# Moving some matmul operands to other start addresses in SBUF, relative to the weights loaded beside them

## The chip, the core and the metric

The kernel runs on one core of a Trainium2 chip. The metric is the device time of one execution in microseconds (us). The engines are called PE (TensorE, matmuls), DVE (VectorE), ACT (ScalarE), POOL (GpSimd) and SP (SyncE, which here only issues DMAs). "PEld" is the part of TensorE that loads weights: each matmul first has its stationary operand (128 columns) loaded, and while one matmul streams its moving operand, the weights of the next are already being loaded. All of it is read from SBUF, 128 partitions wide; an address below is a byte address within a partition.

## The reference

One layer of a decoder trunk, sequence 512, width 1024, 16 heads of 64, all in float32:

```
hn = rms_norm(x); proj = hn @ w_in                     # 1024 -> 3462 columns: q, k, v, forget logits, gate
q, k = rms_norm per head
o_moba = block-sparse attention (4 heads)              # y_moba = rms_norm(o)
cum    = cumsum(log_sigmoid(f_logit))                  # forget sums, 6 heads
o_fox  = softmax(q k / 8 + cum_q - cum_k) v (6 heads)  # y_fox = rms_norm(o) * sigmoid(gate)
o_dil  = mixture of three dilated windows (6 heads)    # y_dil = rms_norm(o)
x = x + concat(y_moba, y_fox, y_dil) @ w_out
x = x + square(relu(rms_norm(x) @ w_up)) @ w_down      # 1024 -> 4096 -> 1024
```

## The kernel before

Every product keeps float32 accuracy by splitting each operand into a rounded part ("hi", type fp32r) and the rest ("lo"). A product is then three matmuls per tile pair: hi by hi, hi by lo, lo by hi. The class `Stream` brings the weights in by DMA (`wraw`, or `ublk` for the up blocks), and `split_group` makes `whi` on ACT (L118) and `wlo` on DVE (L119), two pieces ahead of use.

There are four stages on PE, in this order.

- **In projection and attention** (10 to 236 us of the span). `product` (L274) multiplies x, split into `xh` and `xl`, with nine column chunks of `w_in`. Here x is the stationary operand (128 tokens at a time) and `whi` or `wlo` is the moving one, 512, 256, 262 or 384 columns wide. Between its matmuls a planner puts the steps of the attention heads: transposes (L495, L541, L580), scores (L514, L519), values (L565). DVE and ACT do the softmax and the splits.
- **Out projection** (L274 too). The weights `whi`, `wlo` are stationary and the normed attention outputs move, 512 columns: `y0h`/`y0l`, `y1h`/`y1l`, `y2h`/`y2l` for the three groups.
- **First block of the up projection** (`up0`, L274): the weights are stationary, `zh`/`zl` (the normed-to-be x) move, 512 columns.
- **The MLP** (L872 and L913, 315.7 to 634 us). For seven further blocks of the up projection the kernel uses seven products instead of eight on quarters of 256 columns (a Strassen scheme): products 1, 2, 3 and 4 move a quarter of `zh`/`zl`, products 5, 6 and 7 move a sum of quarters, `t5h`/`t5l`, `t6h`/`t6l`, `t7h`/`t7l`. Each product is 24 matmuls in `up_product` (L872). Between them stand the items of the down projection, `down_item` (L913): 24 matmuls of 512 columns which move `h`, the squared activations, as `hh0`, `hl0`, `hh1`, `hl1`. One round is: product 1, product 5, item, 2, 6, item, 3, 7, item, 4, item. There are seven rounds and then the last items alone: 28 products on `zh`/`zl` (672 matmuls), 21 on the sums (504) and 32 items (768).

The order of instructions on PE is the order in which the code is written. Tiles come from pools (`tile_pool`). A pool on the left takes addresses upward after the pools still open there, a pool with `side="right"` downward from the top. So the start of each tile follows from the sizes of all tiles opened before it. Forget sums: `cumulate` transposes the log gates, scans them along the sequence into the tile `cum` (6 partitions of 512, 2048 bytes of every partition) and writes them to DRAM; `bias_tiles` reads one row back for each of the six heads, spread over 128 partitions, into a tile `ck` of a pool with two buffers.

Of the kernel before, what the change touches and what calls it, by code (L numbers as in the profile page):

```python
# [11 lines left out]
F32 = mybir.dt.float32  # L12
# [6 lines left out]
P = 128  # L19
D = 1024  # L20
S = 512
# [4 lines left out]
NFOX = 6  # L26
# [130 lines left out]
def hymba_block(ctx: ExitStack, tc: tile.TileContext, a, out):  # L157
# [4 lines left out]
    small = ctx.enter_context(tc.tile_pool(name="small", bufs=2))  # L162
# [5 lines left out]
    def bank(tag):  # L168
        return psum.tile([P, 512], F32, name=tag, tag=tag)
# [77 lines left out]
    def product(first, ks, operands, banks_n, done, G=2):  # L247


        n = len(ks)  # L250
        acc = [None] * banks_n
        head, tail = list(range(min(G, n))), list(range(max(G, n - G), n))
        mid = [k for k in range(n) if k not in head and k not in tail]
        order = [(k, b) for b in range(banks_n) for k in head]
        order += [(k, b) for k in mid for b in range(banks_n)]
        order += [(k, b) for b in range(banks_n) for k in tail]
        if first == 0:

            wh, wl = w.take(0)
            acc = [bank("acc") for _ in range(banks_n)]  # L260
            for m in (0, 2, 1):
                for b in range(banks_n):
                    pairs, view = operands(ks[0], b, wh, wl)
                    lhs, rhs = pairs[m]
                    nc.tensor.matmul(view(acc[b]), lhsT=lhs, rhs=rhs, start=(m == 0), stop=False)
            order = [(k, b) for k, b in order if k > 0]
        for k, b in order:
            wh, wl = w.take(first + k)
            if acc[b] is None:
                acc[b] = bank("acc")  # L270
            pairs, view = operands(ks[k], b, wh, wl)
            dst = view(acc[b])
            for m, (lhs, rhs) in enumerate(pairs):
                nc.tensor.matmul(  # L274
                    dst, lhsT=lhs, rhs=rhs, start=(k == 0 and m == 0), stop=(k == n - 1 and m == 2)
                )
            if k == n - 1:
                done(b, acc[b])
            yield
# [11 lines left out]


    p1 = ExitStack()
    xpool = p1.enter_context(tc.tile_pool(name="xpool", bufs=1))
    tokp = p1.enter_context(tc.tile_pool(name="tokp", bufs=5))
    att_stack = ExitStack()
    att = att_stack.enter_context(tc.tile_pool(name="att", bufs=2, side="right"))
# [156 lines left out]
    def cumulate():  # L454
        pt = bank("m")
        for u in range(NT):
            nc.tensor.transpose(out=pt[:NFOX, u * P : (u + 1) * P], in_=lf[:, u], identity=ident)
        cum = small.tile([NFOX, S], F32, name="cum", bufs=1)
        one = ones[:NFOX, :1].broadcast_to([NFOX, S])
        nc.vector.tensor_tensor_scan(cum, one, pt[:NFOX], 0.0, op0=ALU.mult, op1=ALU.add)  # L460
        nc.gpsimd.dma_start(cum_d, cum)
# [177 lines left out]
    for h in range(16):  # L639
        if h % 4 == 0:  # L640
            i = h // 4
            step(("root", i, 0), qk_parts[i][1], [(("qk", i), "root")])
            for t in range(NT):
                step(("norm", i, t), partial(qk_parts[i][2], t), [(("root", i, 0), "zero")] + ([(("norm", i, t - 1), "each")] if t else []))
        for m in range(2):
            needs = [(("norm", h // 4, t), "qk") for t in range(NT)] + [(("s", h - 3, i), "free") for i in range(NT)]
            if h >= FOX0:
                needs.append((("f", 0, 0), "zero"))
            step(("stack", h, m), stack_step(h, m), needs)
        for i in range(NT):  # L650
            needs = [(("stack", h, m), "stack") for m in range(2)] + [(("pt", h - 2, b), "free") for b in range(3)]
            if h >= FOX0:
                needs.append((("f", 0, 0), "cum"))
            step(("s", h, i), s_step(h, i), needs)
        for b in range(3):
            needs = [(("s", h, i), "s") for i in {i for _, i in BANKS[b]}] + [(("av", h - 1, 1), "free")]
            step(("pt", h, b), pt_step(h, b), needs)
        for half in range(2):
            needs = [(("pt", h, b), "pt") for b in range(3)] + [(("v", h // 4), "v")]
            step(("av", h, half), av_step(h, half), needs)  # L660
        step(("o", h, 0), o_step(h), [(("av", h, 1), "av"), (("o", h - 1, 0), "free")])
        if h + 1 == GROUPS[0][1]:
            for t in range(NT):
                step(("y", 0, t), partial(y_transpose, 0, t), [(("o", h, 0), "norm")])
        if h == 15:
            step(("sig", 0, 0), gate, [(("s", 15, NT - 1), "zero"), (("g", 0), "zero")])
        if h == FOX0 - 2:
            step(("f", 0, 0), cumulate, [(("v", 2), "f")])
# [53 lines left out]
    for k in range(0, NK, 2):  # L722
        nc.sync.dma_start(
            x2[:, k : k + 2], a["xT"][k * P : (k + 2) * P, :].rearrange("(k p) t -> p k t", p=P)
        )
    p2 = ExitStack()
    ypool = p2.enter_context(tc.tile_pool(name="ypool", bufs=1))
    for g in (1, 2):
        yT[g] = [ypool.tile([P, 3, S], F32R, name=f"y{g}{m}") for m in "hl"]
# [60 lines left out]


    tp = ctx.enter_context(tc.tile_pool(name="tsums", bufs=1))
    HALF = S // 2
    lo4, hi4, t0, t1 = slice(0, 4), slice(4, 8), slice(0, HALF), slice(HALF, S)
    zop = {1: (zh[:, lo4, t0], zl[:, lo4, t0]), 2: (zh[:, hi4, t0], zl[:, hi4, t0]), 3: (zh[:, hi4, t1], zl[:, hi4, t1])}
    tsum = {}

    def t_sum(n):
        t = mlp_pools["sum"].tile([P, 4, HALF], F32, name="wsum")
        first, second = {  # L800
            5: (zf[:, lo4, t1], zf[:, lo4, t0]),
            6: (zf[:, hi4, t1], tsum.get(5)),
            4: (zf[:, hi4, t0], tsum.get(6)),
            7: (zf[:, hi4, t1], zf[:, lo4, t1]),
        }[n]
        nc.vector.tensor_tensor(t, first, second, op=ALU.subtract)
        tsum[n] = t
        if n == 4:

            hi, lo = zh[:, lo4, t1], zl[:, lo4, t1]  # L810
        else:
            hi, lo = (tp.tile([P, 4, HALF], F32R, name=f"t{n}{m}") for m in "hl")
        zop[n] = (hi, lo)
        return n

    def t_split(n):
        hi, lo = zop[n]
        nc.scalar.copy(hi, tsum[n])
        nc.vector.tensor_tensor(lo, tsum[n], hi.bitcast(F32), op=ALU.subtract)
# [15 lines left out]
    def h_tiles(u):  # L835
        for p in range(2):
            h_at[u, p] = [hp.tile([P, 2, S], F32R, name=f"h{m}{p}", bufs=2) for m in "hl"]

    def square(c, hi, lo, rows=None):

        nc.vector.scalar_tensor_tensor(c, c, 0.0, c, op0=ALU.max, op1=ALU.mult)
        if rows is not None:
            nc.vector.tensor_tensor(c, c, rows, op=ALU.mult)
        nc.scalar.copy(hi, c)
        nc.vector.tensor_tensor(lo, c, hi.bitcast(F32), op=ALU.subtract)
# [13 lines left out]
    def up_product(u, n):  # L859
# [8 lines left out]
        for f in range(2):  # L868
            for j in range(4):
                lh, ll = (x[:, j, f * P : (f + 1) * P] for x in (wh, wl))  # L870
                for m, (lhs, rhs) in enumerate(((lh, bh[:, j]), (lh, bl[:, j]), (ll, bh[:, j]))):
                    nc.tensor.matmul(  # L872
                        acc[:, f * HALF : (f + 1) * HALF], lhsT=lhs, rhs=rhs,
                        start=first and (f, j, m) == (0, 0, 0), stop=(f, j, m) == (1, 3, 2), skip_group_check=True,
# [9 lines left out]
    def up_parts(u, n, acc):  # L884
# [10 lines left out]
        hi, lo = (x[:, :, cols] for x in h_at[u, p])  # L895
        rows = rv[:, cols].unsqueeze(1).broadcast_to([P, 2, HALF]) if u == 7 else None
        square(c.rearrange("p (f t) -> p f t", f=2), hi, lo, rows)
# [30 lines left out]
    for n, _ in enumerate(product(up0_first, list(range(NK)), up_operands, 4, up_done)):  # L928
        if n in (8, 13, 18):
            m = {8: 5, 13: 6, 18: 7}[n]  # L930
            t_sum(m), t_split(m)
        if n == 20:
            t_sum(4)
            zstack.close()
            hp = ctx.enter_context(tc.tile_pool(name="hp", bufs=1, side="right"))
            h_tiles(0)
    t_split(4)
    for u in range(1, 9):
        if u < 8:
# [80 lines left out]
```

## Time and profile before

| | us |
|---|---|
| median of 3 runs | 640.49 (640.24 to 640.78) |
| the profiled execution, its own time | 639.8 |
| its span, first to last instruction | 638.0 |
| PE busy in it | 627.6 |
| DVE busy | 460.2 |
| ACT busy | 322.4 |

[...]

### The profile page before, as it was taken

Reading aid. Unit: us, or ns where it says so; the run is one execution under the profiler, and the core shown is the slowest. Engines: PE = TensorE matmul, PEld = TensorE weight load, DVE = VectorE, ACT = ScalarE, POOL = GpSimd, SP = SyncE. Lnnn points to the kernel's source line nnn. Section 1 sums busy time; section 2 is a strip of 40 time slices with the busy share of each in tenths; the row PEclk is TensorE's granted clock in tenths of the full one; section 3 lists DMA queues with packets and bytes.
Section 4 is the critical chain, followed back from the end, with each engine's and each line's share of the span. In section 5 each row is a group of like instructions: output and inputs, shape, how many; then the busy total and the mean of one; then the engine's idle time right before and its main releaser. Section 6 shows DMA issues by size and latency. Waiting matters only on the chain.

```text
span 638.0 us, 9834 instructions
## 1 busy us (share of the span) xinstructions
PE 627.6 (98%) x3800; PEld 556.3 (87%) x3800; DVE 460.2 (72%) x786; ACT 322.4 (51%) x575; POOL 43.9 (7%) x63
## 2 busy tenths in 40 slices
PE   7999999999999999999999999999999999999997
PEld 5798898898889998888888989898988989988986
DVE  6794695696688565678899676686578765966872
ACT  7457666676777575549543433343434343433320
POOL 4010210130120100002100000000000000000000
PEclk9999999999999999999999999999999999999999
DMA  8524423323422345167425233422530333212213
GB/s 313 161 96 133 123 84 76 125 75 116 134 63 71 106 136 155 51 230 175 107 72 164 84 111 100 131 68 67 166 100 22 144 100 133 66 37 64 67 43 123
DMA packets 24911, 70.03 MB, mean 110 GB/s; under 512 B 3210, under 2 KB 4762, under 8 KB 24864
## 3 DMA queue, kind: packets, MB, share of 16 engines
q1 hardware_dynamic: 18224, 57.84, 28.5%
q10 hardware_dynamic: 4432, 5.77, 3.7%
q0 software_dynamic: 2208, 5.79, 3.7%
q8 instruction: 30, 0.49, 0.3%
q14 instruction: 17, 0.14, 0.1%
HBM read 61.51 MB, written 2.11 MB: 100 GB/s over the span
## 4 chain that ended last, share of the span: by engine, by line
PE 77%; DVE 7%; ACT 1%; issue 1%; ACTq 0%; POOL 0%; DVEq 0%
PE acc L913 28%; PE m L872 22%; PE acc L274 20%; PE m L514 2%; PE m L565 2%; PE m L541 1%; DVE ptl L548 1%; PE m L495 1%; DVE qkss L400 1%; DVE wlo L119 1%; DVE qks L418 1%; DVE m L526 1%; DVE qkraw L413 1%; DVE qkv L401 1%; DVE osum L582 0%
## 5 line engine op out<-in xcount | busy, mean ns | idle before, releaser
L118 ACT CAST whi<-wraw 128x1024 fp32r<-128x1024 f32 (+3 forms) x66 | 66.7, 1014 | 90.5 <-PE acc L913 39.9
L274 PE MATMUL acc<-whi,xh 128*128 128x512 f32 (+3 forms) x284 | 103.4, 364 | 0.7 <-DVE fl L436 0.4
L913 PE MATMUL acc<-hh,wlo 128*128 128x512 f32 x256 | 101.5, 396 | 0.0
L913 PE MATMUL acc<-hh,whi 128*128 128x512 f32 x256 | 101.3, 396 | 0.0
L913 PE MATMUL acc<-hl,whi 128*128 128x512 f32 x256 | 101.2, 395 | 0.0
L119 DVE TENSOR_TENSOR wlo<-wraw,whi 128x1024 fp32r<-128x1024 f32 (+3 forms) x66 | 78.8, 1195 | 29.6 <-ACT whi L118 28.9
L274 PE MATMUL acc<-wlo,xh 128*128 128x512 f32 (+3 forms) x284 | 95.7, 337 | 2.2 <-DVE wlo L119 2.2
L274 PE MATMUL acc<-whi,xl 128*128 128x512 f32 (+3 forms) x284 | 95.8, 337 | 0.0
L872 PE MATMUL m<-zh,whi 128*128 128x256 f32 x224 | 62.5, 279 | 0.0
L872 PE MATMUL m<-zl,whi 128*128 128x256 f32 x224 | 62.3, 278 | 0.0
L872 PE MATMUL m<-zh,wlo 128*128 128x256 f32 x224 | 62.3, 278 | 0.0
L274 PEld LDWEIGHTS acc<-wlo,xh 128*128 128x128 f32 x284 | 54.0, 190 | 5.3 <-DVE wlo L119 3.0
L274 PEld LDWEIGHTS acc<-whi,xl 128*128 128x128 f32 x284 | 53.6, 189 | 5.1
L913 PEld LDWEIGHTS acc<-hh,wlo 128*128 128x128 f32 x256 | 48.3, 189 | 11.0 <-DVE wlo L119 0.3
L913 PEld LDWEIGHTS acc<-hl,whi 128*128 128x128 f32 x256 | 48.3, 189 | 10.3 <-issue 0.2
L913 PEld LDWEIGHTS acc<-hh,whi 128*128 128x128 f32 x256 | 48.3, 189 | 10.1 <-ACT m L882 0.2
L274 PEld LDWEIGHTS acc<-whi,xh 128*128 128x128 f32 x284 | 53.7, 189 | 3.7 <-DVE vs L430 0.7
L922 DVE TENSOR_TENSOR x<-acc,x 128x512 f32<-128x512 f32 (+1 forms) x65 | 42.6, 676 | 10.3 <-PE acc L913 9.6
L118 ACT CAST whi<-wsum 128x1024 fp32r<-128x1024 f32 x28 | 29.4, 1049 | 40.1 <-PE m L872 40.1
L119 DVE TENSOR_TENSOR wlo<-wsum,whi 128x1024 fp32r<-128x1024 f32 x28 | 34.2, 1221 | 19.6 <-ACT whi L118 19.6
L528 ACT ACTIVATE p<-m,mn 128x128 f32<-128x128 f32 (+1 forms) x64 | 33.6, 527 | 24.6 <-DVE mn L526 22.9
L872 PEld LDWEIGHTS m<-zh,whi 128*128 128x128 f32 x224 | 42.1, 188 | 1.2
(193 smaller groups left out, 1323.5 us busy)
## 6 DMA issues: line engine op xcount, KB each, us to landing
wraw<-in_w_down SPq DMA_DIRECT2D x32, 512.0 KB, 3.6
ublk<-in_w_up SPq DMA_DIRECT2D x28, 512.0 KB, 3.8
wraw<-in_w_in SPq DMA_DIRECT2D x21, 512.0 KB, 3.8
stk<-stk ACTq DMA_DIRECT2D x32, 128.0 KB, 2.4
wraw<-in_w_out SPq DMA_DIRECT2D x6, 512.0 KB, 4.1
alibi<-in_alibi POOLq DMA_DIRECT2D x10, 256.0 KB, 3.0
x<-in_xT SPq DMA_DIRECT2D x4, 512.0 KB, 5.5
wraw<-in_w_up SPq DMA_DIRECT2D x4, 512.0 KB, 5.1
```

Source lines behind the costliest of these rows:

```text
L118: nc.scalar.copy(hi, raw)
L119: nc.vector.tensor_tensor(lo, raw, hi.bitcast(F32), op=ALU.subtract)
L274: nc.tensor.matmul(dst, lhsT=lhs, rhs=rhs, start=(k == 0 and m == 0), stop=(k == n - 1 and m == 2))
L400: nc.vector.tensor_reduce(ss, sq.rearrange("p (h d) -> p h d", d=DH), axis=AX.X, op=ALU.add)
L401: nc.vector.tensor_scalar(state["v"][:, t], ss, 1.0 / DH, eax[:, t : t + 1], op0=ALU.mult, op1=ALU.add)
L413: nc.vector.tensor_tensor(raw, raw, state["y"][:, t].unsqueeze(2).broadcast_to([P, 8, DH]), op=ALU.mult)
L514: nc.tensor.matmul(ps[:, :n], lhsT=st[0][:, i * P : (i + 1) * P], rhs=st[m][:, :n], start=(m == 1), stop=(m == 2 and h < FOX0),)
L528: nc.scalar.activation(p, ps[:, :n], AF.Exp, bias=mn, scale=-1.0, accum_out=st["den"][:, i : i + 1])
L565: nc.tensor.matmul(ot[:, j * P :], lhsT=v, rhs=p, start=(half == 0 and j == 0), stop=(half == 1 and j == 3))
L872: nc.tensor.matmul(acc[:, f * HALF : (f + 1) * HALF], lhsT=lhs, rhs=rhs, start=first and (f, j, m) == (0, 0, 0), stop=(f, j, m) == (1, 3, ...
L913: nc.tensor.matmul(acc, lhsT=lhs, rhs=rhs, start=(p, k, m) == (0, 0, 0), stop=(p, k, m) == (1, 1, 2))
L922: nc.vector.tensor_tensor(dst[:, cols], acc[:, cols], dst[:, cols], op=ALU.add)
```

## The change

No instruction is added, removed or moved: on every engine the order of operations is the same before and after. Tiles start elsewhere. Four small tiles that nothing writes or reads (`edgex`, `edgey`, `edget`, `edgeh`: 256, 256, 192 and 320 bytes of each partition) are put ahead of other tiles, and the tile `cum` goes: the sums are scanned into the first buffer of `ck`, which gives 2048 bytes back. Heads 10 to 15 then take the two buffers of `ck` in the other order. In the pool `hp` the tiles `m1`, `m5`, `m6` (kept products) are opened ahead of `c` (the tile that is squared).

```
@@ ahead of xpool
+    p1.enter_context(tc.tile_pool(name="edgex", bufs=1)).tile([P, 64], F32, name="edgex")
     xpool = p1.enter_context(tc.tile_pool(name="xpool", bufs=1))
@@ cumulate
-        cum = small.tile([NFOX, S], F32, name="cum", bufs=1)
+        cum = att.tile([P, S], F32, name="ck")[:NFOX]
@@ ahead of ypool
     p2 = ExitStack()
+    p2.enter_context(tc.tile_pool(name="edgey", bufs=1)).tile([P, 64], F32, name="edgey")
     ypool = p2.enter_context(tc.tile_pool(name="ypool", bufs=1))
@@ the pool of the sums of quarters
     tp = ctx.enter_context(tc.tile_pool(name="tsums", bufs=1))
+    tp.tile([P, 48], F32, name="edget")
@@ the pool of h, after the first h_tiles
             h_tiles(0)
+            for m in (1, 5, 6):
+                hp.tile([P, S], F32, name=f"m{m}", bufs=1)
+            hp.tile([P, 80], F32, name="edgeh")
```

What this does to the distance, in bytes modulo 512, between a moving operand and the weights that are loaded while it streams (worked out from the tile starts of the two built programs; a column is 4 bytes):

| stage | stationary | moving | before | after |
|---|---|---|---|---|
| in projection, 512, 256 and 384 columns | xh, xl | whi, wlo | 0 | 256 |
| in projection, 262 columns | xh, xl | whi, wlo | 0, 24, 48 | 256, 280, 304 |
| out projection, group 0 | whi, wlo | y0 | 64 | 64 |
| out projection, groups 1 and 2 | whi, wlo | y1, y2 | 0 | 256 |
| up0, and products 1 to 4 | whi, wlo | zh, zl | 64 | 64 |
| products 5 to 7 | whi, wlo | t5, t6, t7 | 0 | 192 |
| down items | whi, wlo | hh, hl | 64 | 256 |

The attention's own operands keep their places. Among them, the second score matmul of a forgetting head (L514) streams at 256 from the weights of L519, which are loaded beside it, before and after.

## Rows read from the trace of the kernel before

**Rows 1.** The page: busy time, share of the span and instructions of PE and DVE.
```profile
PE 627.6 (98%) x3800; PEld 556.3 (87%) x3800; DVE 460.2 (72%) x786; ACT 322.4 (51%) x575; POOL 43.9 (7%) x63
```

**Rows 2.** The chain that ended last, share of the span by engine (page).
```profile
PE 77%; DVE 7%; ACT 1%; issue 1%; ACTq 0%; POOL 0%; DVEq 0%
```

**Rows 3.** That chain in order of time, by lines, then start, time, work; one MLP round.
```profile
by line: PE acc L913 27.9%; PE m L872 21.8%; PE acc L274 19.8%; PE m L514 1.8%; PE m L565 1.7%; PE m L541 1.3%; issue 1.1%; DVE ptl L548 1.1%; PE m L495 1.0%; DVE qkss L400 0.8%; DVE wlo L119 0.7%; DVE qks L418 0.7%; DVE m L526 0.6%; DVE qk
...
359.59 5.60 PE m L872 x48
365.19 5.60 PE acc L913 x24
370.80 5.71 PE m L872 x48
376.50 5.60 PE acc L913 x24
382.11 5.71 PE m L872 x48
387.82 5.60 PE acc L913 x24
393.42 2.83 PE m L872 x24
396.25 5.51 PE acc L913 x24
401.75 5.60 PE m L872 x48
```

**Rows 4.** Busy time by engine and granted clock in the MLP, 315.6 to 606.8 us.
```profile
315.60:606.80 291.20, 291.20 (x1829) 261.81 (x1829) 218.83 (x255) 112.90 (x137) 0.00 (x0) 1.00 0.30 93
```

**Rows 5.** Who waited for whom, total us, times, longest; ACT's waits for PE.
```profile
ACT whi L118 <- PE m L872: 73.0, 47, 1.9
ACT whi L118 <- PE acc L913: 51.7, 21, 4.4
```

**Rows 6.** The timeline of PE (start us, duration us), 256 columns: zh, sums, zh later.
```profile
359.43 0.28 PE L872 MATMUL m<-zh,whi 128*128 128x256 f32 x1
...
362.04 0.28 PE L872 MATMUL m<-zh,wlo 128*128 128x256 f32 x1
...
362.39 0.28 PE L872 MATMUL m<-t5h,wlo 128*128 128x256 f32 x1
...
364.91 0.28 PE L872 MATMUL m<-t5h,wlo 128*128 128x256 f32 x1
...
381.94 0.28 PE L872 MATMUL m<-zh,whi 128*128 128x256 f32 x1
...
384.65 0.28 PE L872 MATMUL m<-zh,wlo 128*128 128x256 f32 x1
```

**Rows 7.** The timeline of PE, 512 columns: in projection, then two down items.
```profile
23.83 0.39 PE L274 MATMUL acc<-whi,xl 128*128 128x512 f32 x1
...
25.87 0.39 PE L274 MATMUL acc<-whi,xl 128*128 128x512 f32 x1
...
353.93 0.40 PE L913 MATMUL acc<-hh,whi 128*128 128x512 f32 x1
...
356.45 0.39 PE L913 MATMUL acc<-hh,wlo 128*128 128x512 f32 x1
...
369.00 0.40 PE L913 MATMUL acc<-hh,wlo 128*128 128x512 f32 x1
...
370.40 0.40 PE L913 MATMUL acc<-hh,wlo 128*128 128x512 f32 x1
```

**Rows 8.** Groups of PE's matmuls by line and form: xcount | busy, mean ns | idle before.
```profile
L913 PE MATMUL acc<-hh,wlo 128*128 128x512 f32 x256 | 101.5, 396 | 0.0
...
L274 PE MATMUL acc<-wlo,xh 128*128 128x512 f32 x124 | 48.7, 393 | 2.2 <-DVE wlo L119 2.2
...
L274 PE MATMUL acc<-wlo,xh 128*128 128x256 f32 x96 | 27.1, 282 | 0.0
...
L872 PE MATMUL m<-t5h,wlo 128*128 128x256 f32 x56 | 15.8, 283 | 0.0
```

**Rows 9.** The timeline of PE: two score matmuls, 512 columns, and the mask behind them.
```profile
181.72 0.62 PE L514 MATMUL m<-stk,stk 128*128 128x512 f32 x2
182.18 0.22 PE L519 MATMUL m<-diag,identr 128*128 128x128 f32 x1
```

**Rows 10.** The timeline of PE: a chunk of 256 columns of the in projection.
```profile
36.98 0.28 PE L274 MATMUL acc<-whi,xh 128*128 128x256 f32 x1
...
38.78 0.28 PE L274 MATMUL acc<-whi,xh 128*128 128x256 f32 x1
```

**Rows 11.** The chain in the attention stage, three of its pieces around 130 us.
```profile
128.88 1.06 DVE ptl L548 x2
129.94 0.60 DVE osum L582
130.53 0.59 DVE qkss L400
```

**Rows 12.** The copy of the forget sums: DMA to DRAM, start us (view of the tile).
```profile
L461 POOL DMA_DIRECT2D cum_d<-cum x1: 532/532/532, 160.9 to 160.9; - x1
```

More of the change, by code (lines that the diff above doesn't have):

```diff
@@ L293, in hymba_block @@
     p1 = ExitStack()
+    p1.enter_context(tc.tile_pool(name="edgex", bufs=1)).tile([P, 64], F32, name="edgex")
     xpool = p1.enter_context(tc.tile_pool(name="xpool", bufs=1))
@@ L457, in cumulate @@
             nc.tensor.transpose(out=pt[:NFOX, u * P : (u + 1) * P], in_=lf[:, u], identity=ident)
-        cum = small.tile([NFOX, S], F32, name="cum", bufs=1)
+        cum = att.tile([P, S], F32, name="ck")[:NFOX]
         one = ones[:NFOX, :1].broadcast_to([NFOX, S])
@@ L726, in hymba_block @@
     p2 = ExitStack()
+    p2.enter_context(tc.tile_pool(name="edgey", bufs=1)).tile([P, 64], F32, name="edgey")
     ypool = p2.enter_context(tc.tile_pool(name="ypool", bufs=1))
@@ L792, in hymba_block @@
     tp = ctx.enter_context(tc.tile_pool(name="tsums", bufs=1))
+    tp.tile([P, 48], F32, name="edget")
     HALF = S // 2
@@ L936, in hymba_block @@
             h_tiles(0)
+            for m in (1, 5, 6):
+                hp.tile([P, S], F32, name=f"m{m}", bufs=1)
+            hp.tile([P, 80], F32, name="edgeh")
     t_split(4)
```

## The prediction

> **What bounds the kernel now.** I read the page first: PE is busy for 627.6 of 638.0 us [rows 1], and the chain that ended last lies on PE for 77% of the span and on DVE for 7% [rows 2]. [...]
>
> [...] By the timeline, 256 columns on zh go at (362.04 - 359.43) / 23 = 113.5 ns in one product and at (384.65 - 381.94) / 23 = 117.8 ns in another; on the sums of quarters it is (364.91 - 362.39) / 21 = 120.0 ns [rows 6]. Column count, weights, clock and engine are the same. For 512 columns it is (25.87 - 23.83) / 9 = 226.7 ns in the in projection, (356.45 - 353.93) / 11 = 229.1 in one down item and (370.40 - 369.00) / 6 = 233.3 in another [rows 7]. The steps between these are alike: 120.0 - 113.5 = 6.5 and 233.3 - 226.7 = 6.6 ns. So a matmul pays one fixed delay of about 6.6 ns, or does not, or pays it in one of three or two of three. Each stretch locks into one of these paces and keeps it to its end. What distinguishes zh from the sums is where they lie: 64 and 0 bytes, modulo 512, from their weights. I read the delay as a collision between the moving operand and the weights loaded beside it. Distance 0 is bad for 256 columns (120.0) and good for 512 (226.7); distance 64 is mixed for both. So distance matters together with length and with the moment at which a stretch begins, and the trace has no long stretch at 256 or 192.
>
> **The change part by part.** The *sums of quarters* go from 0 to 192: 504 matmuls (nine forms of 56 [rows 8]), now 120.0 ns. If they reach the best pace seen, 113.5, that saves 504 x 6.5 = 3.3 us, all on the path. Bounds: 0 (they stay at the worst pace seen) and 3.3. I take 3.3, since at 120.0 they pay the delay on every matmul today, and two of the three paces seen lie below.
>
> The *down items* go from 64 to 256: 768 matmuls (three forms of 256 [rows 8]) on 27.9% of 638.0 us = 178.0 us, 231.8 ns each [rows 3]. At 226.7 they take 174.1 us: 3.9 less. At 233.3 throughout they take 179.2: 1.2 more. The rows nearest in distance are the scores, whose second matmul streams at 256: two matmuls of 512 columns in 182.18 - 181.72 = 0.46 us, 230 each [rows 9]; that is one pair amid other work, not a stretch that had time to lock. I take 226.7 and keep both ends.
>
> The *in projection* goes from 0 to 256. Its 288 matmuls of 256 columns (three forms of 96 [rows 8]) run at (38.78 - 36.98) / 15 = 120.0 ns [rows 10]; 6.5 ns less on each is 1.9 us. Not all of that is on the path, since DVE steps stand in the chain of this stage [rows 11] and a faster PE only waits longer for them. I take half, 0.9; bounds 0 and 1.9. Its 372 matmuls of 512 columns (three of 124 [rows 8]) settle at 226.7 today where nothing disturbs them [rows 7], so there is nothing to win, and up to 372 x 6.6 = 2.5 us, half of it on the path, 1.2, to lose. I take 0. The *out projection's* 144 matmuls on y1 and y2 lie at 0 as well: 0 taken, 144 x 6.6 = 1.0 at worst.
>
> The *products on zh*, 672 matmuls, keep their distance. But the pace they lock into depends on when they begin, and that moves. In the round shown, one product of four is at 113.5 and the others at 117.8 (a pair with a sum takes 5.60 or 5.71 us [rows 3]). All at 117.8 costs 168 x 4.3 = 0.7 us, all at 113.5 saves 504 x 4.3 = 2.2. I take 0.
>
> The *tile of the forget sums* costs nothing: the copy to DRAM starts at 160.9 us [rows 12], the heads that read it back must wait for it anyway, and the buffer it now shares is not wanted before that. The split of zl gains a wait for that DMA, over a hundred microseconds after it is done. If that cover were gone, DVE would stand there with the rest of zl's split queued behind, and PE's up0 behind that. The new order of m and c in hp changes which old tile's memory they take over; both are written after the last reader of that memory, and PE does not read them. Nobody reads the four empty tiles.
>
> Sum: -3.3 - 3.9 - 0.9 = -8.1 on the profiled execution's own 639.8 us: 631.7. That execution lies 0.7 below the median of the runs, 640.49, so on that scale 632.4. With all lower bounds (3.3 + 3.9 + 1.9 + 2.2 = 11.3) it is 629.2.
>
> What is late next if PE is this much faster? A round takes 401.75 - 359.59 = 42.16 us; 8.1 us less over the whole kernel is some 1.1 us a round, under 3%. DVE at 218.83 of 291.20 us [rows 4] has a quarter to spare, so the weights still come in time.
>
> **Rivals.** *A: the delay is only thinned out.* At the new distances the stretches lock into the mixed paces, 117.8 and 229.1, as zh and some down items do today [rows 6, 7]. Then the sums save 504 x 2.2 = 1.1, the down items 768 x 2.7 = 2.1 and the in projection 0.3: 3.5 us, 637.0. For it: two of the four stretches that I timed at 64 are at such a pace. Against: distances far from both 0 and 64 may well be clear.
>
> *B: nothing.* The paces are set by the moment of the start and not by the distance, or the distance counts in another measure than modulo 512. Each stretch draws a pace as before: 640.5. For it: at the same distance of 64, down items run at 229.1 and at 233.3, and the score pair at 256 is no faster. Against: every stretch on the sums that I looked at goes at 120.0 and those on zh never do.
> [...]
>
> *C: slower.* Distance 256 is a bad one for 512 columns, as 64 is for most down items and 0 is not. The down items, the in projection's and the out projection's wide matmuls all lock at 233.3: +1.2, +1.2, +1.0, and zh falls to 117.8 throughout, +0.7, with the sums unchanged at 120.0: +4.1, so 644.6. For it: y and the in projection leave 226.7, the best pace there is, for an unknown one. The sign turns where the wide matmuls' loss passes what the 256-column ones gain: with the sums at 113.5 even all of C's wide losses (3.4) only just cancel 3.3.
>
> [...]
> [...]
>
> **How the numbers follow.** The forecast, 632.4, has 0.42; A (637.0) 0.25; B (640.5) 0.15; C (644.6) 0.13; D (625.6) 0.05. The low end of the range is the forecast with all lower bounds, 629.2, and a little for half of D's mixtures: 628.5. The high end takes in B with its own scatter and a mild C: 641.5. About 0.2%, 1.3 us, is what a measurement of this kernel can tell from no change. Faster by more than that: forecast, A and D, 0.72, less 0.01 for weak cases of A: 0.71. Within it: B, 0.15. Slower: C, with that hundredth, 0.14.
>
> **What would show it.** Products 5 to 7: starts 113.5 ns apart, pairs of products 5.4 to 5.6 us and not 5.71. Down items: pieces of 5.44 us (24 x 226.7) where 5.60 stood. The in projection's 256-column stretch: below 120.0. If the sums still start 120.0 apart, the distance is not the cause; if they speed up and the down items slow to 5.60 everywhere, C has its half. It would be wrong altogether if durations on DVE or ACT change, since nothing here should touch them, or if PE begins to wait for wlo in the MLP.

## The result, and the profile after

The changed kernel takes 636.12 us, median of three runs (636.07 to 636.59), against 640.49 before: a ratio of 0.9935 with a 95% interval of 0.9922 to 0.9948, 4.4 us less. It is faster, by less than the forecast's 8.1 and within the stated range of 628.5 to 641.5.

The profiled execution took 636.59 us with a span of 634.8. The first view is again the chain that ended last in order of time, one round of the MLP (start, time held, work); L876 is L872 of before, L917 is L913. It answers to [rows 3].

```profile
359.95 5.65 PE m L876 x48
365.61 5.44 PE acc L917 x24
371.05 5.65 PE m L876 x48
376.70 5.44 PE acc L917 x24
382.14 5.65 PE m L876 x48
387.80 5.44 PE acc L917 x24
393.23 2.83 PE m L876 x24
396.06 5.48 PE acc L917 x24
```

Three of the four down items of a round take 5.44 us where they took 5.60, and the fourth 5.48 for 5.51. The pairs of products take 5.65 each, where two took 5.71 and one 5.60: the sums gained, and the one zh product of the round that had been fast lost. All seven rounds read like this one, but for the first item of round 1 (5.61) and of round 5 (5.55). By the chain, the MLP goes from 316.48 to 631.38 us, 314.9 us; before it went from 315.82 to 634.58, 318.8.

The timeline of PE (start, duration) answers to [rows 6, 7, 10]: a product on zh, one on the sums, a down item, and the 256-column chunk of the in projection.

```profile
359.79 0.28 PE L876 MATMUL m<-zh,whi 128*128 128x256 f32 x1
...
362.50 0.28 PE L876 MATMUL m<-zh,wlo 128*128 128x256 f32 x1
...
362.86 0.28 PE L876 MATMUL m<-t5h,wlo 128*128 128x256 f32 x1
...
365.33 0.28 PE L876 MATMUL m<-t5h,wlo 128*128 128x256 f32 x1
...
376.54 0.39 PE L917 MATMUL acc<-hh,whi 128*128 128x512 f32 x1
...
381.75 0.39 PE L917 MATMUL acc<-hh,wlo 128*128 128x512 f32 x1
...
36.84 0.28 PE L274 MATMUL acc<-whi,xh 128*128 128x256 f32 x1
...
38.64 0.28 PE L274 MATMUL acc<-whi,xh 128*128 128x256 f32 x1
```

In this timeline a matmul of 256 columns is recorded with 0.28 us and one of 512 with 0.39, while the next starts about 0.12 or 0.23 us after it: the records overlap. So what a stretch costs is taken from start to start: the difference of two start times, divided by the matmuls between them. A piece of the chain is the sum of such steps (24 x 226.7 ns = 5.44 us).

The zh product starts a matmul every (362.50 - 359.79) / 23 = 117.8 ns, the sums every (365.33 - 362.86) / 21 = 117.6, the down item every (381.75 - 376.54) / 23 = 226.5, the in projection every (38.64 - 36.84) / 15 = 120.0. So the wide matmuls of the down items reach the best pace seen before (226.7); the sums go from the worst (120.0) to the middle one (117.8); and the in projection, whose distance went from 0 to 256, did not change by a nanosecond (120.0 before).

The rest of the kernel is where it was, except for one thing: the MLP begins 0.7 us later than in the profile of before. In this execution the granted clock was lower at the start, 0.87 where it was 1.00 (stretch, then busy time by engine; the clock is the number behind POOL's; before, then after). That this is the cause is not shown: over the fourteen profiles of this case the first matmul of the MLP starts between 315.7 and 317.6 us, and the latest of them, `e9_entry`, had a clock of 1.00 at its start. The other two timed runs of the changed kernel, at a clock of 1.00, have spans of 634.3 us, 0.5 less than the profiled one.

```profile
0.00:10.00 10.00, 6.95 (x29) 5.85 (x29) 3.93 (x7) 5.72 (x10) 3.80 (x9) 1.00 0.83 283
...
0.00:10.00 10.00, 6.41 (x24) 5.62 (x25) 3.70 (x6) 5.64 (x9) 3.56 (x9) 0.87 0.84 282
```

### The profile page after: what moved, and what is told of

Read it like the earlier page. It is cut to its first block, busy times and chain, and to the rows that moved or that the text cites. A ratio compares the mean times of both kernels' runs of the same rounds, so it can differ in the third digit from the quotient of the medians.

```text
span 634.8 us, 9834 instructions
## 1 busy us (share of the span) xinstructions
PE 625.1 (98%) x3800; PEld 556.0 (88%) x3800; DVE 459.6 (72%) x786; ACT 322.6 (51%) x575; POOL 43.9 (7%) x63
## 4 chain that ended last, share of the span: by engine, by line
PE 76%; DVE 7%; ACT 1%; issue 1%; DMA 1%; ACTq 0%; POOL 0%; DVEq 0%
PE acc L917 28%; PE m L876 22%; PE acc L274 19%; PE m L516 2%; PE m L567 2%; PE m L543 1%; DVE ptl L550 1%; PE m L497 1%; DMA stk<-stk 1%; DVE qkss L402 1%; DVE wlo L119 1%; DVE qks L420 1%; DVE m L528 1%; DVE qkraw L415 1%; DVE qkv L403 1%
## 5 line engine op out<-in xcount | busy, mean ns | idle before, releaser
L917 PE MATMUL acc<-hh,whi 128*128 128x512 f32 x256 | 100.2, 391 | 0.0
L917 PE MATMUL acc<-hh,wlo 128*128 128x512 f32 x256 | 99.9, 390 | 0.0
L917 PE MATMUL acc<-hl,whi 128*128 128x512 f32 x256 | 99.6, 389 | 0.0
L876 PE MATMUL m<-zh,whi 128*128 128x256 f32 x224 | 62.8, 280 | 0.0
L876 PE MATMUL m<-zh,wlo 128*128 128x256 f32 x224 | 62.6, 279 | 0.0
L876 PE MATMUL m<-zl,whi 128*128 128x256 f32 x224 | 62.5, 279 | 0.0
L917 PEld LDWEIGHTS acc<-hh,wlo 128*128 128x128 f32 x256 | 48.0, 188 | 10.6 <-DVE wlo L119 0.5
L917 PEld LDWEIGHTS acc<-hl,whi 128*128 128x128 f32 x256 | 48.1, 188 | 9.2 <-issue 0.2
L917 PEld LDWEIGHTS acc<-hh,whi 128*128 128x128 f32 x256 | 48.1, 188 | 9.1 <-issue 0.2
L876 PEld LDWEIGHTS m<-zh,whi 128*128 128x128 f32 x224 | 42.0, 188 | 1.1
```

Of the source, the lines that this page charges most:

```text
L876: nc.tensor.matmul(acc[:, f * HALF : (f + 1) * HALF], lhsT=lhs, rhs=rhs, start=first and (f, j, m) == (0, 0, 0), stop=(f, j, m) == (1, 3, ...
L917: nc.tensor.matmul(acc, lhsT=lhs, rhs=rhs, start=(p, k, m) == (0, 0, 0), stop=(p, k, m) == (1, 1, 2))
```

## The experiments

In what follows, a **pace** is the distance from start to start once a stretch has settled, read from the timeline over the last 12 matmuls of a product or item. There are 28 products on zh, 21 on the sums and 31 items between them that are read so in each run. All kernels but the last start from the changed one; an added tile of n words moves what lies beyond it by 4n bytes. The runs `e7` to `e10` and `e12` were timed once only, so of them the paces count and not the time.

### Other places modulo 128

The first question was what "distance" is: to the weights or absolute, and modulo what. After the result a simple story was open. The moving operands in question start at 32 or 96 modulo 128, before and after; h went from 96 to 32 and gained, the sums went from 32 to 96 and gained, and the in and out projections stayed in their class and did not change. So a period of 128 bytes, or the moving operand's own start without any part of the weights, explained everything as well as the distance did.

Run `e1_start0`, all three moving operands at new places:

```
     rv = mlp.tile([P, S], F32, name="rv")
+    mlp.tile([P, 24], F32, name="edgez")
-    tp.tile([P, 48], F32, name="edget")
+    tp.tile([P, 24], F32, name="edget")
-            hp.tile([P, 80], F32, name="edgeh")
```

> The changed kernel with zh, the sums and h moved to starts that are 0 modulo 128 (zh at 384, sums at 0, h at 384 modulo 512; weights still at 416). Theories: (1) the distance to the weights modulo 512 decides; all are now at 96 or 480, near 0 and 64, so paces between those seen: sums and zh 117 to 120 ns, h 229 to 233, 636 to 641 us. (2) the distance modulo 128 decides and (3) the moving operand's own start modulo 128 decides, the weights do not matter: both say that this is a class never seen (starts were 32 or 96 modulo 128 so far), so any pace; if a start on a 128-byte boundary saves one read per matmul, zh and the sums go under 113 ns and h under 226 ns, 625 us or less.

Measured: 642.45 us, ratio to before 1.0036 (1.0022 to 1.0050). h at 233.3 in all 31 items, the sums at 120.0 in all 21 products, zh at 118.2 in 27 of 28. The starts on a 128-byte boundary saved nothing here; these are bad places. The paces are those that theory 1 gave, the time is above its 641.

Run `e2_start64` is the same edit with 8 words for zh and 8 for the sums.

> The changed kernel with zh, the sums and h all at 448 modulo 512 (64 modulo 128), weights at 416. Theory 1 (distance modulo 512): 32 from the weights, between 0 and 64, so paces as seen at those, 636 to 641 us. Theories 2 and 3 (distance or own start modulo 128): a new class; if only the 64-byte boundary counts, the same paces as with starts at 0 modulo 128; if 128 bytes count, zh and sums differ from that run by about 6.6 ns per matmul (7.8 us over 1176 matmuls).

Measured: 640.54 us, ratio 0.9997 (0.9986 to 1.0008). h at 233.3 throughout. zh at 116.7 in 15 products and 117.8 in 13, the sums at 116.7 in 12 and 117.8 in 9. So at a distance of 32 there is a pace of 116.7 that no other distance showed, and the 64-byte boundary is no gain either.

Run `e3_weights64` moves the weights and leaves zh, the sums and h where they are:

```
+    ctx.enter_context(tc.tile_pool(name="edgew", bufs=1)).tile([P, 16], F32, name="edgew")
     splits = ctx.enter_context(tc.tile_pool(name="splits", bufs=3))
-    tp.tile([P, 48], F32, name="edget")
+    tp.tile([P, 32], F32, name="edget")
```

> The changed kernel with the weights' tiles and everything on the left above them moved up by 64 bytes, while zh, sums and h keep their absolute starts (480, 96, 160). Theory 1 (distance modulo 512): h at 192, sums at 128, zh at 0 from the weights: zh goes to 120 ns as the sums were at distance 0 (+1.4 us), in projection unchanged, since its distance stays 256. Theory 2 (distance modulo 128): h is at 64, sums and zh at 0: h back to 229 to 233 ns (+2 to +5 us), sums and zh 120 ns (+2.5 us), in projection unchanged; 641 us or more. Theory 3 (own start of the moving operand modulo 128): h stays at 226.7, sums and zh at 117.8; but whi and wlo, which move in the in projection, go from 32 to 96: their 256 columns fall from 120 to 117.8 or 113.3 ns, their 512 columns rise from 226.7 to 229 to 233.

Measured: 642.96 us, ratio 1.0038 (1.0019 to 1.0058). The chain of one of its rounds and of its last five items, and those of the changed kernel (here L877 and L918 are the products and the items, there L917 the items):

```profile
366.18 5.61 PE acc L918 x24
371.79 5.72 PE m L877 x48
377.51 5.60 PE acc L918 x24
...
609.57 28.02 PE acc L918 x120
...
604.11 27.25 PE acc L917 x120
```

h has the same addresses as in the changed kernel and goes from 226.7 back to 233.3 in all 31 items; zh, now at distance 0, goes to 120.0 in all 28 products, as the sums did at distance 0; the sums, now at 128, go to 119.0. In the in projection the moving operand's own start changed class and the distance did not: its 256-column matmuls still start 120 ns apart in the median. Theory 3 falls: the weights' place counts. Theory 1's forecast for zh is exact. Moving a tile also moves where DVE, ACT or a DMA writes it, and no run was made to part the two. The last five items speak against ACT and DVE: in the changed kernel ACT does nothing from 618 to 625 us and DVE is busy for 1.86 of these 7 us, and the items still keep 226.7, as those of `e3_weights64` keep 233.3 to the end.

The first block of the up projection, `up0`, moves zh with 512 columns and shows the same from the other side. In the timeline, first of the changed kernel, then of `e3_weights64`:

```profile
311.29 0.39 PE L274 MATMUL acc<-zh,wlo 128*128 128x512 f32 x1
...
315.41 0.39 PE L274 MATMUL acc<-zh,wlo 128*128 128x512 f32 x1
...
311.25 0.39 PE L275 MATMUL acc<-zh,whi 128*128 128x512 f32 x1
...
315.33 0.39 PE L275 MATMUL acc<-zh,whi 128*128 128x512 f32 x1
```

At distance 64 it runs at (315.41 - 311.29) / 18 = 228.9 ns, at distance 0 at (315.33 - 311.25) / 18 = 226.7. So one move of the weights slowed h and sped up `up0`, each to a pace that its new distance has elsewhere: h at 192 takes the 233.3 that `up0` takes in `e11_mirror`, where zh was moved to 192 and the weights were not. That supports the distance, and not the weights' own place, as what counts.

Run `e4_other512` puts h at 32 and the sums at 224 (80 words for `edget`, 112 for `edgeh`).

> The changed kernel with the sums at 224 and h at 32 modulo 512: distances 320 and 128 instead of 192 and 256, but the same places modulo 128 (96 and 32). Theory 1 (modulo 512): the paces change, by up to 6.6 ns a matmul on 504 and 768 (some 3 to 5 us in all, either way). Theories 2 and 3 (modulo 128): nothing changes: h 226.7, sums 117.8, 636.1 us within 1 us.

Measured: 640.47 us, ratio 1.0002 (0.9990 to 1.0013). h, at distance 128, left 226.7 and runs at 231.7 to 232.9; its pieces in the chain are 5.59 where they were 5.44:

```profile
365.51 5.59 PE acc L917 x24
371.09 5.65 PE m L876 x48
376.75 5.59 PE acc L917 x24
```

Theory 2 falls too: 128 is not the period. The sums, at 320, stayed at 117.8, as at 192. With h about at its pace of before (231.8 in the prediction's sum) the gain on h is gone, and the total is that of before.

### The period is 256

Now 0 and 256 looked alike for every operand (120.0 for 256 columns, 226.7 for 512), so 256 bytes could be the period and "256 away" the same as "0 away". Run `e5_half_period` moves each operand by another 256:

```
+    mlp.tile([P, 64], F32, name="edgez")
-    tp.tile([P, 48], F32, name="edget")
+    tp.tile([P, 112], F32, name="edget")
```

> The changed kernel with h at distance 0 instead of 256, the sums at 448 instead of 192 and zh at 320 instead of 64: each 256 bytes further on. Theory P256 (the distance counts modulo 256, so that 0 and 256 are the same): h stays at 226.7 ns, sums and zh at 117 to 118; 636.1 us within 1. Theory P512 (distance counts modulo 512, 256 is clear and 0 is not): h returns to 229 to 234 ns, +2 to +5 us, 638 to 641.

Measured: 636.71 us, ratio 0.9946 (0.9931 to 0.9961). h at 226.7 in all 31 items, sums and zh at 117.8 in all. Its round in the chain repeats the changed kernel's:

```profile
360.19 5.65 PE m L877 x48
365.85 5.44 PE acc L918 x24
371.29 5.65 PE m L877 x48
```

P256 holds, P512 falls. Run `e6_only_h` leaves out the edges ahead of x, y and the sums:

> The changed kernel without the edges ahead of x, y and the sums: h alone is moved (distance 256), the sums and the in projection are back at 0. Both theories: h 226.7 as in the changed kernel, sums 120.0 as before: 636.1 + 504 x 2.4 ns = 637.3 us. In projection and out projection: P256 says no difference at all from the changed kernel, P512 allows one.

Measured: 638.23 us (637.51 to 639.21), ratio 0.9968 (0.9959 to 0.9978), 0.9 us over the forecast, with runs that spread over 1.7. h at 226.7 (30 of 31), the sums at 120.0, as forecast. The 288 matmuls of 256 columns of the in projection take 36.7 us from start to start in before, in the changed kernel and here, and the 72 on y2 take 16.3 us in all three: the edges ahead of x and y do nothing, as P256 says.

Run `e7_map` filled three gaps (88 words for `edgez`, 40 for `edget`, 32 for `edgeh`):

> The changed kernel with distances never tried: h at 96, sums at 160, zh at 224. If for 512 columns 0 modulo 256 alone is clear, h is at 233 to 234 ns (+5 us); if clearness grows with the distance from 0, h at 96 lies near the clear pace. For 256 columns 0 is the worst pace seen (120.0): sums and zh should lie below it, at 117 to 119.

Measured: 641.97 us in one run. h at 96: 233.3 in all 31, so clearness does not grow with the distance. Sums at 160: 117.1 (20 of 21); zh at 224: 118.2 in 27 and 118.8 in one product. That last is the very count of `e1_start0`, where zh lay at 480, which is 224 + 256.

All paces together, by distance modulo 256 (ns; two values where stretches of one run differ; without `e8_lo_pair` and `e10_hl_only` below, in which one stretch has several distances; the paces of single stretches that stand apart are left out):

| distance mod 256 | 256 columns | 512 columns, h and `up0` |
|---|---|---|
| 0 | 120.0 | 226.7 |
| 32 | 116.7, 117.8 | 233.3 |
| 64 | 113.3, 117.8 | 228.9, 233.3 |
| 96 | 120.0 | 233.3 |
| 128 | 119.0 | 231.7 to 232.9 |
| 160 | 117.1 | not tried |
| 192 | 113.3, 117.8 | 233.3 |
| 224 | 118.2 | 233.3 |

The distance that is clear for 512 columns, 0, is one of the two worst for 256. Only in `e3_weights64` was the distance changed by moving the weights, in all other rows of the table by moving the other operand.

### Which weights

Run `e8_lo_pair` asked whether a moving operand collides with the weights of the matmul that follows, which load meanwhile, or with those it is multiplied by:

```
         hi = self.split_pool.tile([P, 1024], F32R, name="whi")
+        if not self.parts:
+            self.split_pool.tile([P, 16], F32, name="edgew", bufs=1)
         lo = self.split_pool.tile([P, 1024], F32R, name="wlo")
...
-            h_at[u, p] = [hp.tile([P, 2, S], F32R, name=f"h{m}{p}", bufs=2) for m in "hl"]
+            hh = hp.tile([P, 2, S], F32R, name=f"hh{p}", bufs=2)
+            if not u:
+                hp.tile([P, 16], F32, name=f"edgel{p}", bufs=1)
+            h_at[u, p] = [hh, hp.tile([P, 2, S], F32R, name=f"hl{p}", bufs=2)]
+            if not u:
+                hp.tile([P, 112], F32, name=f"edgem{p}", bufs=1)
```

> The changed kernel with wlo moved up 64 bytes against whi, and hl moved up 64 bytes against hh. Theory NEXT (a moving operand collides with the weights of the following matmul, which load while it streams): hh streams beside whi, hl beside wlo, hh beside the next whi, all at distance 256: down items stay at 226.7 ns. Theory OWN (the weights that it is multiplied with count): hl by whi is at 320, hh by wlo at 192, two of three matmuls off: 229 to 234 ns, +2 to +5 us on the down items. The in projection changes too here (distances 192 and 256 in turn) and is read apart.

Measured: 639.04 us in one run. The down items settle at 231.1 (30 of 31 at 231.1 or 231.2); in the chain they are pieces of 5.53 us:

```profile
371.15 5.66 PE m L883 x48
376.81 5.53 PE acc L924 x24
```

NEXT, taken alone, falls: every moving operand had the weights loaded beside it at a clear distance and the pace was still not 226.7. (That the weights of a matmul load while the one before it streams can be read from the timeline: in the changed kernel the load for the matmul at 376.76 us is recorded from 376.54 on, when the matmul before it starts.) In the in projection of this run, with distances 192 and 256 in turn, matmuls of 256 columns start 118.0 ns apart in the median instead of 120.0. For the down items, 231.1 is what two delays in three would give, (226.7 + 2 x 233.3) / 3, which suits OWN; but it also suits a third story, that a change of place from one moving operand to the next costs, since two of the three steps change. Run `e10_hl_only`, with the second half of that edit alone, was to set these apart:

> The changed kernel with hl alone moved up 64 bytes (hh, whi and wlo as in the changed kernel). Of the three matmuls of a down triple, one is then off the clear distance, whether the weights loaded beside it (hl beside wlo) or its own (hl by whi) count: one delay of 6.67 ns in three, 228.9 ns at most. Theory STEP (a change of place modulo 256 from one moving operand to the next also costs): two of three steps change, 231.1 ns, as in the run in which wlo and hl were both moved.

Measured: 637.87 us in one run. The down items settle at 231.8 or 231.9 (29 of 31), well over the 228.9 that one operand off its distance allows. So neither NEXT nor OWN suffices, and STEP, near to it, is 0.7 ns short. What the collision is between stays open. The run had a second finding. Its chain:

```profile
365.03 5.56 PE acc L922 x24
370.59 5.55 PE m L881 x48
376.14 5.56 PE acc L922 x24
381.70 5.55 PE m L881 x48
```

The pairs of products fell from 5.65 to 5.55, although neither zh nor the sums nor any weights moved: 15 of the 21 products on the sums settled at 113.3 instead of 117.8. Of what PE does, only what ran before them had changed.

### The moment of entry

Run `e9_entry` puts that to the test: the first matmul of each product is cut in two along its columns, at another column in each round.

```
+    CUT = {1: 0, 2: 128, 3: 64, 4: 192, 5: 32, 6: 224, 7: 96}
...
+                    edges = (0, HALF) if (f, j, m) != (0, 0, 0) or not CUT[u] else (0, CUT[u], HALF)
+                    for e0, e1 in zip(edges, edges[1:]):
                         nc.tensor.matmul(
-                            acc[:, f * HALF : (f + 1) * HALF], lhsT=lhs, rhs=rhs,
+                            acc[:, f * HALF + e0 : f * HALF + e1], lhsT=lhs, rhs=rhs[:, e0:e1],
```

> The changed kernel, where in rounds 2 to 7 of the MLP the first matmul of each up product is cut in two along its columns (128 and 128, 64 and 192, 192 and 64, 32 and 224, 224 and 32, 96 and 160; round 1 uncut): the same work, one more weight load, another moment for all that follows. Theory DISTANCE ALONE: after the first matmuls every product on zh and on the sums settles at 117.8 ns in every round, and the cuts only cost: up to 50 ns a product, 42 products, +2 us. Theory ENTRY (distance offers several paces, the moment of entry picks one): in some of the rounds products settle at 113.3 ns, 24 x 4.4 = 0.1 us less per product.

Measured: 642.09 us in one run. The timeline of round 5 (cut at 32), first zh, then the sum:

```profile
488.66 0.28 PE L879 MATMUL m<-zh,whi 128*128 128x256 f32 x1
...
491.02 0.28 PE L879 MATMUL m<-zh,wlo 128*128 128x256 f32 x1
491.13 0.38 PE L879 MATMUL m<-t5h,whi 128*128 128x32 f32 x2
...
491.71 0.28 PE L879 MATMUL m<-t5l,whi 128*128 128x256 f32 x1
...
493.75 0.28 PE L879 MATMUL m<-t5l,whi 128*128 128x256 f32 x1
```

zh goes on at (491.02 - 488.66) / 20 = 118.0 ns, the sum at (493.75 - 491.71) / 18 = 113.3, at the distance of 192 at which it runs at 117.8 in round 1. In rounds 5 and 6 (cuts at 32 and 224) all six products on the sums settle at 113.3; in the other rounds and on zh nothing does. ENTRY holds, for the sums: the same addresses offer two paces, and what happens at the entry picks one, which then holds to the end. Between these rounds only the cut differs; the distances are the same. As a tool it is too dear: a cut product takes 2.84 to 2.86 us at 113.3 and 2.93 or 2.94 at 117.8, against 2.83 uncut, so that a cut costs about 0.1 us, twice the 50 ns of the expectation, which were an estimate of the author's that no run shows.

Run `e11_mirror` (96 words for `edgez`, 16 for `edget`, 112 for `edgeh`) tried other places, in the hope of a faster version:

> The changed kernel with zh at distance 192 and the sums at 64 (the changed kernel has them at 64 and 192); h stays at 256. If the paces belong to the distance and the moment of entry, both offer 113.3 and 117.8 ns to 256 columns, and which is taken cannot be told: all at 117.8 gives 636.1 us, zh at 113.3 throughout 633.1, the sums at 113.3 throughout 633.9, both 630.9; up0, which moves zh at 512 columns, may lose up to 0.4. If the distance alone set the pace, 636.1 within 1 us.

Measured: 637.01 us, ratio 0.9949 (0.9935 to 0.9962). All products at 117.8, h at 226.7 (29 of 31); `up0`, at 192 instead of 64, lost 0.4 us (96 matmuls in 22.6 instead of 22.2). So it cannot tell the two readings of its expectation apart. None of these placements beat the changed kernel.

### Fewer weights

Run `e12_fewer_weights` starts from the kernel before, with h at 64:

```
-                    nc.tensor.matmul(acc, lhsT=lhs, rhs=rhs, start=(p, k, m) == (0, 0, 0), stop=(p, k, m) == (1, 1, 2))
+                    n = P if (p, k, m) in ((0, 0, 0), (1, 1, 2)) else {2: 64, 4: 64, 5: 32}.get(q, P)
+                    nc.tensor.matmul(acc[:n], lhsT=lhs[:, :n], rhs=rhs, start=(p, k, m) == (0, 0, 0), stop=(p, k, m) == (1, 1, 2))
```

> The kernel before (h at distance 64), where in down items of rounds 3 and 5 ten of the twelve matmuls per output tile load 64 columns of weights instead of 128, and in round 6 32 columns; the other rows of those products are left out. [...]

It asks whether the reading of the weights beside the moving operand has a part in the delay. If it has, the narrowed items should come to 226.7 or near it, the more the fewer columns; if not, they should keep the 228.9 or 233.3 of the others.

Measured: 640.09 us in one run. The chain, items of rounds 2, 3, 4 and 6 (128, 64, 128 and 32 columns):

```profile
389.00 5.60 PE acc L914 x24
...
430.78 5.48 PE acc L914 x24
...
472.78 5.60 PE acc L914 x24
...
545.27 5.58 PE acc L914 x24
```

With 64 columns all eight items settle at 228.3 ns and none at 233.3, where in before 19 of all 32 items did; one of them holds a longer step near its start. With 32 columns the four settle at 232.4 to 233.2. So the width of the weights has a part in the pace. That it is their reading is not shown: the matmul then also writes fewer rows of its result (`acc[:n]`). And fewer columns are not simply less delay: the fourth item of round 6, with 32, is slower than its like with 128 (228.9). No stretch went below 226.7. What that pace is made of stays open.

## Why the prediction held, and where it missed

**The bound** was read rightly. In the MLP nothing but PE is on the chain, before and after [rows 3]; before, PE was busy there for 291.20 of 291.20 us at a granted clock of 1.00 [rows 4], and ACT, which makes the weights, waited for PE [rows 5]. So a nanosecond less per matmul is a nanosecond less of time there, and what the matmuls lost the kernel lost: 318.8 - 314.9 = 3.9 us in the MLP. The medians differ by 4.4 and the two profiled spans by 3.2; the difference lies in when the MLP begins and in the spread of the runs.

**The down items**, taken from 231.8 to 226.7 ns for 3.9 us: right. From start to start in the timeline they take 3.5 us less (by the chain 27.5% of 634.8 = 174.6 us instead of 178.0). The rest is in items that take longer than 24 x 226.7 ns = 5.44 us: the fourth of each round, 5.48, and one of 5.55. The row that I set aside, the score pair at 256 with 230 each [rows 9], was no guide: stretches at 256 settle at 226.7.

**The sums of quarters**, taken from 120.0 to 113.5 for 3.3 us: the term that was most mis-sized. They went to 117.8 for 1.2, about rival A's price (1.1). The mistake is in the step "if they reach the best pace seen", a choice by distance alone. `e9_entry` and `e10_hl_only` show that 113.3 exists at this distance and that the entry decides. The two bounds, no gain and 3.3, held; the value between them could not be read from the trace of before.

**The in projection**, taken at 0.9: nothing came, rival B's price, for a reason that could have been seen as a question: the distance went from 0 to 256, and the trace could not tell a period of 512 from one of 256. `e5_half_period` and `e6_only_h` settle it. The out projection, taken at 0, is 0 for the same reason, and the loss of C could not occur.

**The zh products**, taken at 0: 0.8 lost, about the bound given (0.7). In the trace of before, eight zh products follow a down item that settles at 228.8 or 228.9 and seven of them are fast; of the others none is [rows 3, 6]. With the items of the changed kernel at 226.7 none is fast. The step said that the entry picks the pace; it was then applied to zh and not to the sums.

By the starts in the timeline the terms measured are -3.5 - 1.2 + 0.8 = -3.9 where -8.1 stood. Of the signs named beforehand, the pieces of 5.44 came; starts 113.5 apart on the sums and less than 120.0 in the in projection did not, and the pairs of products, 5.65, lie outside the 5.4 to 5.6 given. That the time lies in the stated range is therefore no proof of the sum: the range also held the time of before, and of three gains one came nearly whole, one by a third and one not at all. The tile of the forget sums, the order in `hp` and the wait of zl cost nothing that shows, as forecast: DVE is busy for 459.6 us after and 460.2 before [rows 1].

**The rivals.** None came alone. The forecast holds for h, A for the sums, B for the in projection. The total lies nearest to A's 637.0, which is in part luck: A had 2.1 for h, which gained 3.5, 0.3 for the in projection, which gained nothing, and no loss on zh. C is not what happened, but wide matmuls do lock at 233.3 at a bad distance: at distances of 192, 224, 32 and 96 h runs at 233.3 throughout, and with zh and the sums in bad places too the kernel takes 642 to 643 us (`e1_start0`, `e3_weights64`). D supposed that the best paces hold a delay themselves. No run shows the term behind its 625.6, of which the low end of the range, 628.5, has a part: in the twelve runs no stretch settled below 226.7 or 113.3. Against B, and for a part of the weights in the running matmul's pace, stands `e3_weights64`: of the MLP's operands it moved nothing but the weights, and the pace of h went from 226.7 to 233.3.

## What to carry to other kernels

Where PE is the bound and a long stretch of equal matmuls does not run at its best pace, read the distance between starts in the timeline and compare stretches that differ only in operand addresses; a pad of less than 256 bytes moved a settled pace by 2 to 3% here (the sums from 120.0 to 117.8 by the 192 bytes of `edget`, h from 226.7 to 233.3 by the 64 bytes of `edgew` in `e3_weights64`). Find out the period before spending pads: here 256 bytes, so that 0 was as good as 256 for h (226.7 at both), and the edges ahead of x and y did nothing (36.7 and 16.3 us with and without them). The best place differed with the number of columns (distance 0: 226.7 for 512, the best, and 120.0 for 256, the worst), and a stretch locked into a slower or a faster pace by the way it was entered (117.8 or 113.3 at one distance, `e9_entry`), so each such change has to be measured as a whole.

## What was not expected of the hardware

- Paces came in steps: 113.3, 117.8 and 120.0 ns for 256 columns, 226.7, 228.9 and 233.3 for 512 stood out, one delay of 6.67 ns apart or thirds of it. Other distances gave paces between these (116.7, 118.2, 119.0; 231.7), and one distance can offer two. Within one run all stretches of a kind mostly took the same one (31 of 31 items at 226.7 and 28 of 28 products on zh at 117.8 in `e5_half_period`).
- The clear distance for 512 columns, 0 modulo 256 (226.7), is with 96 the worst tried for 256 columns (120.0).
- A stretch's pace depended on what ran before it: 15 of 21 products on the sums went from 117.8 to 113.3 when hl was moved (`e10_hl_only`), though hl is not among their operands.
- With h at 64, half of the weight columns brought 228.3 ns, a quarter of them 232.4 to 233.2 (`e12_fewer_weights`).
- Open: which weights, or which change of place, a moving operand collides with, and what the best paces, 226.7 and 113.3, are made of.
